# Stage Y of a decoder layer's MLP: Strassen's seven products for the up-projection, in two rounds of 612 tokens

## Chip, core and metric

One NeuronCore of a Trainium2 chip runs the whole program. It has five engines with an instruction stream each: PE (TensorE, matrix products), DVE (VectorE), ACT (ScalarE), POOL (GpSimd) and SP, which here issues nearly all DMAs. The metric is device time in microseconds (us) for one execution; lower is better. All operands and results are fp32.

## What is computed

One decoder layer over 2048 prompt tokens and 8 sample tokens, T = 2056 in all, D = 1024, d_ff = 4096. Attention, pooling and the sample group's caches come first; they are not touched. What matters here is the rest, the same for every token:

```python
hp = hp + _mixer_out(outs, lses, pooled, w_out)        # [A, B] @ w_out
def _mlp(h, g, w_up, w_down):
    a = jax.nn.relu(rmsnorm(h, g) @ w_up)
    return (a * a) @ w_down
hp = hp + _mlp(hp, norm_mlp_g, w_up, w_down)
def _ple(h, p, g, w_gate, w_ple):
    gate = jax.nn.sigmoid(rmsnorm(h, g) @ w_gate)
    return (p @ w_ple) * gate
hp = hp + _ple(hp, p_prompt, ple_norm_g, w_ple_gate, w_ple)
y_prompt = rmsnorm(hp, final_norm_g)
```

## The kernel before

Activations lie transposed, features on the 128 partitions and tokens along the columns. Every fp32 operand is split into a high part (a cast to fp32r, a format that PE reads) and a low part (the value less its high part), and each product is made of three passes, high x high, high x low, low x high (PASSES). `group` runs the passes over the k tiles into one PSUM bank with `mm` (L190).

After the input projection the tokens are worked in two stages. Stage X holds the first 832 tokens (CX, two chunks of 416); stage Y the last 1224 (CY, chunks of 416, 416 and 392). In the order of the program: the output projection of X, mlp of X with part of the attention in the background, the output projection of Y (with the gate's normalised input of X prepared beside it), the gate of X (with the mlp's normalised input of Y, `prep_norm`, beside it, paced in 24 steps), the mlp of Y (with the final norm, transposes and output of X beside it), the gate of Y and its final norm.

`out_proj` takes each tile of xT into one of two buffers (`xr_`), runs a group of 24 matmuls, adds (DVE, L196), stores h1 to DRAM and adds the square to the statistics.

`mlp` runs 8 blocks of 512 hidden features. A block's upward half has 4 feature tiles x 3 chunks, a group of 8 k tiles x 3 passes = 24 matmuls each: 288; ACT empties the bank with a relu (L1344), POOL squares (L196), ACT casts the high part (L1347), DVE subtracts for the low part (L196). Its downward half has 8 output tiles x 3 chunks, groups of 4 x 3 = 12: 288 again; DVE adds each bank to the accumulator `hacc` in SBUF (L196). Weights come through `load_w`: a DMA of 256 KB into the ring `wr` (SP), POOL copies the high part (`pcopy`, L199), DVE subtracts for the low part (L196). w_up and w_down are read once for all of stage Y.

`gate` makes, for each of 8 output tiles and each chunk, a group of 24 matmuls, the sigmoid, the product with `ple`, the sum in `hacc`, its square for the last norm and the scale by final_norm_g. `Final` transposes on PE (L1466), scales on ACT and DVE (L1472, L1474) and stores the output.

What sets the order: instructions are issued in the order of the code, engine by engine; work in the background is a generator, and `Pace` advances it by so many steps for so much matmul work in front. All memory comes from a few arenas of columns (R for fp32r, F for fp32, and "ma", "mb", which change hands).

## Time and profile before

| | us |
|---|---|
| median of 3 runs | 2733.47 (2732.52 to 2735.83) |
| the profiled execution, own time | 2738.41 |
| its span, first to last instruction | 2736.7 |
| mean granted TensorE clock | 0.988 |
| output projection of Y (span time 1545 to 1651) | 106.0 |
| gate of X (1651 to 1740) | 89.0 |
| mlp of Y (1740 to 2603) | 863.0 |
| gate of Y, up to the last matmuls (2603 to 2724) | 121.0 |

The profile is of one execution. Times of an instruction are its recorded duration; on PE such records overlap, since matmuls are pipelined, so how far apart matmuls stand is read from a row that holds many of them without a break. PEld are the loads of weights into PE, one per matmul. In the table of stages each column is an engine's busy time with its count of instructions, then the granted clock as a share of full speed, the DMA engines' mean busy share, and the GB/s moved.

### The profile page before, as it was taken

How to read it: one execution, taken by the hardware profiler on the slowest of the kernel's cores; microseconds unless marked ns; L12 is line 12 of the kernel's file. 1: busy time of each engine (PE TensorE's matmuls, PEld its weight loads, DVE VectorE, ACT ScalarE, POOL GpSimd, SP SyncE). 2: the span in 40 equal slices, each digit the busy share in tenths (PEclk: the TensorE clock that was granted, in tenths of full speed). 3: DMA queues.
4: the chain of work that ended last, by engine and by line, in shares of the span. 5: the costliest groups of instructions: out<-in, count | busy, mean ns of one | idle time of the engine just before them, and what ended most of it. 6: DMA issues, size and time to landing. Idle time of an engine off the chain costs nothing. (4 is left out here: it accounts for less than half of the span.)

```text
span 2736.7 us, 43091 instructions
## 1 busy us (share of the span) xinstructions
PE 2654.8 (97%) x15686; PEld 2533.5 (93%) x15686; DVE 1555.8 (57%) x3373; ACT 847.9 (31%) x1605; POOL 1030.3 (38%) x1354
## 2 busy tenths in 40 slices
PE   8999899998999999999999999999999999999998
PEld 6888899977988999999999898999999999999998
DVE  6747766675587766766775757432332332323675
ACT  6221344453243244242343424301011011011354
POOL 2414645444276443343443725412122122122263
PEclk9999999999999999999999999999999999999999
DMA  7364244477144332332322545431111111111124
GB/s 248 127 181 123 80 131 115 112 214 198 55 132 120 88 88 69 109 104 74 95 73 61 165 147 153 131 104 39 39 39 44 42 39 39 39 39 39 53 84 150
DMA packets 385938, 272.51 MB, mean 100 GB/s; under 512 B 91466, under 2 KB 349205, under 8 KB 385717
## 3 DMA queue, kind: packets, MB, share of 16 engines
q1 hardware_dynamic: 385653, 269.74, 34.1%
q8 instruction: 123, 2.02, 0.3%
q14 instruction: 90, 0.74, 0.1%
q10 hardware_dynamic: 72, 0.02, 0.0%
HBM read 209.47 MB, written 60.30 MB: 99 GB/s over the span
## 5 line engine op out<-in xcount | busy, mean ns | idle before, releaser
L190 PE MATMUL bank<-mem_r 128*128 128x416 f32 (+11 forms) x13608 | 2455.9, 339 | 49.7 <-DVE mem_r L196 11.1
L190 PEld LDWEIGHTS bank<-mem_r 128*128 128x128 f32 (+2 forms) x13608 | 2311.1, 185 | 128.3 <-DVE mem_r L196 18.9
L199 POOL TENSOR_SCALAR mem_r<-mem_f 128x512 fp32r<-128x512 f32 (+1 forms) x444 | 324.9, 736 | 808.3 <-PE bank L190 718.3
L196 DVE TENSOR_TENSOR mem_r<-mem_f,mem_r 128x512 fp32r<-128x512 f32 (+3 forms) x568 | 434.1, 770 | 179.4 <-POOL mem_r L199 139.4
L196 DVE TENSOR_TENSOR mem_f<-bank,mem_f 128x416 f32<-128x416 f32 (+3 forms) x488 | 272.6, 565 | 238.0 <-PE bank L190 228.0
L196 DVE TENSOR_TENSOR mem_r<-mem_mb,mem_r 128x416 fp32r<-128x416 f32 (+6 forms) x236 | 173.6, 743 | 339.6 <-ACT mem_r L1347 312.2
L1344 ACT ACTIVATE mem_mb<-bank 128x392 f32<-128x392 f32 (+1 forms) x160 | 82.3, 515 | 798.5 <-PE bank L190 798.5
L196 POOL TENSOR_TENSOR mem_mb<-mem_mb 128x416 f32<-128x416 f32 (+1 forms) x140 | 143.2, 1023 | 307.1 <-ACT mem_mb L1344 282.6
L776 DVE CUSTOM_DVE_ANT_0 bank<-bank,mask 128x256 f32<-128x256 f32 (+3 forms) x504 | 159.5, 338 | 43.5 <-PE bank L190 39.6
L199 POOL TENSOR_SCALAR mem_r<-mem_r 128x256 fp32r<-128x256 f32 (+1 forms) x117 | 91.5, 795 | 87.8 <-PE bank L190 77.7
L859 POOL TENSOR_SCALAR_AFFINE_SELECT mem_ma<-mem_ma 128x256 f32<-128x256 f32 (+2 forms) x148 | 74.7, 524 | 99.4 <-ACT mem_ma L871 44.6
L196 DVE TENSOR_TENSOR mem_ma<-bank,mem_ma 128x416 f32<-128x416 f32 (+2 forms) x104 | 63.4, 610 | 85.6 <-PE bank L190 70.3
L1347 ACT CAST mem_r<-mem_mb 128x416 fp32r<-128x416 f32 (+1 forms) x128 | 68.5, 535 | 134.2 <-POOL mem_mb L196 134.1
L190 PE MATMUL bank<-mem_mb,mem_r 128*64 128x64 f32 (+4 forms) x494 | 99.9, 321 | 3.1 <-DVE mem_r L196 1.0
L190 PEld LDWEIGHTS bank<-mem_mb,mem_r 128*128 128x128 f32 (+1 forms) x494 | 79.4, 177 | 12.3 <-DVE mem_r L196 1.7
L196 DVE TENSOR_TENSOR mem_r<-mem_ma,mem_r 128x512 fp32r<-128x512 f32 (+4 forms) x88 | 70.8, 809 | 32.4 <-ACT mem_r L880 26.1
L199 POOL TENSOR_SCALAR mem_r<-mem_mb 128x512 fp32r<-128x512 f32 (+3 forms) x61 | 57.2, 946 | 70.6 <-PE bank L190 51.4
L196 POOL TENSOR_TENSOR mem_f<-mem_f 128x416 f32<-128x416 f32 (+2 forms) x52 | 69.2, 1334 | 32.0 <-DMA mem_f<-in_cache_attn_kv_dram 12.5
L776 DVE DVE_READ_ACCUMULATOR2_ANT mem_ma<- 128x1 f32 (+1 forms) x512 | 68.4, 134 | 0.0
L196 POOL TENSOR_TENSOR mem_ma<-mem_ma 128x416 f32<-128x416 f32 (+1 forms) x41 | 52.5, 1289 | 38.3 <-ACT mem_ma L1410 14.4
L196 DVE TENSOR_TENSOR mem_f<-mem_f,mem_ma 128x416 f32<-128x416 f32 (+1 forms) x64 | 47.2, 737 | 26.2 <-ACT mem_ma L1190 11.3
L859 POOL TENSOR_SCALAR_AFFINE_SELECT mem_mb<-mem_mb 128x256 f32<-128x256 f32 (+2 forms) x76 | 33.9, 466 | 56.2 <-ACT mem_mb L868 21.2
(254 smaller groups left out, 1808.9 us busy)
## 6 DMA issues: line engine op xcount, KB each, us to landing
mem_f<-in_w_up_dram SPq DMA_DIRECT2D x128, 256.0 KB
mem_f<-in_w_down_dram SPq DMA_DIRECT2D x128, 256.0 KB
mem_f<-in_w_in_dram SPq DMA_DIRECT2D x64, 256.0 KB
out_dram<-mem_f SPq DMA_DIRECT2D x55, 256.0 KB
mem_f<-in_cache_attn_kv_dram SPq DMA_DIRECT2D x48, 256.0 KB
mem_f<-in_w_ple_gate_dram SPq DMA_DIRECT2D x48, 256.0 KB
mem_f<-in_x_prompt_dram SPq DMA_DIRECT2D x64, 128.0 KB
xT_s<-mem_f SPq DMA_DIRECT2D x32, 256.0 KB
```

What stands on the lines that cost most here:

```text
L190: PE.matmul(out, l, r, start=start, stop=stop)
L196: eng.tensor_tensor(out, a, b, op=op)
L199: G.tensor_scalar(out, src, 1.0, 1.0, op0=ALU.mult, op1=ALU.mult)
L776: V.tensor_tensor_reduce(src, src, mask, 1.0, -3e38, ALU.add, ALU.max, mcol[: src.shape[0], col : col + 1])
L859: G.affine_select(out=p, in_=p, pattern=[[0, nblk], [sign, w]], compare_op=ALU.is_ge, fill=0.0, base=base, channel_multiplier=-sign)
L1344: S.activation(a, ps[:, :ln], AF.Relu)
L1347: S.copy(x[:, 0], sq)
```

## The change

The tokens of stage Y are cut into four chunks of 306 (HY) and worked in two rounds of two chunks, 612 tokens each. In a round, the up-projection treats weights and activations as 2 x 2 halves: the k tiles' upper and lower 512 rows, the hidden features' lower and upper 2048, and the two chunks. Instead of eight products of halves it makes seven of sums and differences (Strassen's scheme in Winograd's form; SEVEN lists operand slots, bank, and product). `upward` does this for 128 hidden features of each half: 7 products x 4 k x 3 passes = 84 matmuls of 306 columns, 16 times per round. Three products open a bank and four add to a bank that holds another; after each, ACT copies the bank (4) or DVE adds it (3) into `z`, four results of 306 columns. Relu, square and cast are three ACT instructions of 1224 columns, the low part one of DVE. `downward` is an ordinary product: 4 output tiles x 2 chunks, 12 matmuls each, 96, 16 times per round. The steps follow one another as `sections` lists them.

`Weights7` loads four blocks of 256 x 128 of w_up (4 DMAs of 128 KB), makes the sums on DVE (`w_sums`, 4 of 256 columns), and the parts: ACT casts and DVE subtracts, 1024 columns at once ("early") and 768 ("late"). `WeightsD` loads w_down, one cast and one subtraction of 1024. Both weights are read once per round, twice in all. `Fill` prepares a step's weights while the step before runs.

Around it: the normalised, summed activations are made by `prep_seven`, four steps of 7 slots x 306, beside the gate of X for round 1 and at the end of round 1 for round 2. The gate of X writes its result to DRAM (hxS) and `final_from` reads it back tile by tile in the first upward steps of round 1. Round 1's result goes to DRAM (h2) and is reloaded. The gate of Y is called for chunks (0, 1), (2) and (3), loading its weights each time. COLS_F gives 832 columns to a new piece "mc", which changes which buffers the first stages draw.

The core of the diff:

```diff
@@ constants
-CY = [(2 * LC, LC), (3 * LC, LC), (4 * LC, T - 4 * LC)]
+HY = NY // 4
+CY = [(NX + i * HY, HY) for i in range(4)]
-COLS_F = 10824
+COLS_F = 9992
+COLS_MC = 832
@@ after mlp
+    SEVEN = ((0, 0, 0, 1), (3, 3, 2, 5), (5, 5, 0, 6), (1, 1, 1, 2), (4, 4, 0, 7), (6, 2, 2, 3), (2, 6, 0, 4))
+    OPENS = (1, 2, 5)
+    def w_sums(raw, s):
+        tt(V, s[:, 0], raw[:, 0], raw[:, 3], ALU.subtract)
+        tt(V, raw[:, 3], raw[:, 3], raw[:, 2], ALU.add)
+        tt(V, s[:, 1], raw[:, 3], raw[:, 0], ALU.subtract)
+        tt(V, s[:, 2], raw[:, 1], s[:, 1], ALU.subtract)
...
+        def early(self):
+            w_sums(self.a, self.b)
+            self.p4 = self.parts(self.a, self.w4, 4)
+        def late(self):
+            self.p3 = self.parts(self.b, self.w3, 3)
+        def parts(self, src, ring, n):
+            w = [x.rearrange("p (s n) -> p s n", s=n) for x in ring()]
+            S.copy(w[0], src)
+            tt(V, w[1], src, f(w[0]), ALU.subtract)
+            return w
...
+        for blk in range(NBLK):
+            for j in range(2):
+                out.append((True, blk, j))
+                if blk:
+                    out.append((False, blk - 1, j))
+        return out + [(False, NBLK - 1, j) for j in range(2)]
...
+        def upward(blk, j):
+            ws = fill.take()
+            z = z_view(zr(4 * ln), 4)
+            for slot_w, slot_z, b, p in SEVEN:
+                n, last = 0, 3 * len(x) - 1
+                for k, xk in enumerate(x):
+                    for i, q in PASSES:
+                        PE.matmul(bu[b][:, :ln], ws[k // 2].at(slot_w, i, k % 2), xk[:, q, slot_z],
+                                  start=n == 0 and p in OPENS, stop=n == last, skip_group_check=p not in OPENS)
+                        n += 1
+                fill.work(12 * ln)
+                ps = bu[b][:, :ln]
+                if p in (1, 5, 6, 4):
+                    S.copy(z[:, {1: 0, 5: 2, 6: 3, 4: 1}[p]], ps)
+                else:
+                    i = {2: 0, 3: 3, 7: 2}[p]
+                    tt(V, z[:, i], ps, z[:, i], ALU.add)
+                if p == 3:
+                    fill.late()
+            S.activation(z, z, AF.Relu)
+            S.activation(z, z, AF.Square)
+            r = rl[blk, j] = z_parts_view(rls(), 4)
+            S.copy(r[:, 0], z)
+            tt(V, r[:, 1], z, f(r[:, 0]), ALU.subtract)
+        def downward(blk, half):
+            ws = fill.take()
+            fill.late()
...
+                                mm(ps[:, :ln], ws[o // 2].at(i, 2 * fh + j, o % 2), rl[blk, j][:, q, AT[fh, ci]], n == 0, n == 11)
+                    hc = hacc[ft].ap[:, ci * ln : ci * ln + ln]
+                    tt(V, hc, ps[:, :ln], hc, ALU.add)
...
@@ stage Y
-    gate(xg, hx, stx.buf.ap, (0, 1), gate_w(wr), Pace(bg, 24, 24 * NX * 7))
+    bg = prep_seven(h1, rst, g_mlp, xs, CY[:2], zr)
+    gate(xg, lambda ft, ci: hx[ft].ap[:, ci * LC : ci * LC + LC], stx.buf.ap, (0, 1), gate_w(wr), Pace(bg, 4, 24 * NX * 7), dump=hxS)
-    mlp(xm, get_acc_y, 512, wr, Pace(bg, 7, 24 * NY * 3.5), before_last_y)
+    bgx = final_from(hxS, finx, tpx)
+    fill = Fill(chain(mlp_steps(), mlp_steps()), rings, None)
+    fill.hook = Pace(bgx, 8, 2 * 7 * 12 * HY * 0.9)
+    hy, st1 = mlp_seven(xs, acc_of(h1, slice(y0, y1)), rls, zring, fill, last_1, keep_1)
+    hy2, st2 = mlp_seven(cur["xs"], acc_of(h1, slice(y1, T)), rls, zring, fill, last_2, lambda *_: None)
-    gate(xg, hy, sums[:, :NX], (0, 1), gate_w(wr), Pace(held["bg"], 9, 24 * NX))
+    gate(xg, where, sums.ap, (0, 1), gate_w(wr), Pace(bg, 16, 24 * 2 * HY * 7))
+    gate(xg, where, sums.ap[:, 2 * HY :], (2,), gate_w(wr, w_more), Pace(bg, 7, 24 * HY * 7))
+    last_gate(xg, hy2, y1, where, sums.ap[:, 3 * HY :], 3, gate_w(wr, w_more), Ring.of(wr.b + yr.b),
+              final(hy2, y1, sums.ap[:, 2 * HY :], y1, y1 + HY, yr), 4)
```

How the engines' rows stand, in three places; a row is a line of the code, an operation, what it writes and reads, and how often in a row.

First, DVE in the middle of stage Y's mlp. Before, bank to `mem_f` is the accumulators' sum, 512 columns a weight's low part, `mem_mb` the squared activations' low part:

```order
L196 TENSOR_TENSOR mem_f<-bank_73,mem_f 128x392
L196 TENSOR_TENSOR mem_r<-mem_f,mem_r 128x512
L196 TENSOR_TENSOR mem_f<-bank_70,mem_f 128x392
L196 TENSOR_TENSOR mem_r<-mem_f,mem_r 128x512
L196 TENSOR_TENSOR mem_r<-mem_mb_15973,mem_r 128x416 x2
L196 TENSOR_TENSOR mem_r<-mem_f,mem_r 128x512 x2
L196 TENSOR_TENSOR mem_r<-mem_mb_15973,mem_r 128x392
```

After, in the middle of a round, 256 columns are a sum of weights, 1024 the low part of four slots or of w_down, bank to `mem_ma` an upward product's sum, bank to `mem_f` an accumulator's:

```order
L199 TENSOR_TENSOR mem_f<-bank_77,mem_f 128x306
L199 TENSOR_TENSOR mem_r<-mem_ma_1834,mem_r 128x1224
L199 TENSOR_TENSOR mem_f<-mem_f 128x256
L199 TENSOR_TENSOR mem_f<-bank_75,mem_f 128x306
L199 TENSOR_TENSOR mem_f<-mem_f 128x256 x2
L199 TENSOR_TENSOR mem_r<-mem_f,mem_r 128x1024
L199 TENSOR_TENSOR mem_f<-mem_f 128x256 x4
L199 TENSOR_TENSOR mem_ma_1834<-bank_72,mem_ma_1834 128x306
L199 TENSOR_TENSOR mem_ma_1834<-bank_74,mem_ma_1834 128x306
```

The preparation of the next weights now stands between the banks' sums, in pieces, where before one subtraction of 512 stood between several sums.

Second, PE where stage Y's mlp begins. Before, groups of 24 follow the gate's without a break, with the ones-products of X's statistics and the transposes of X's result (L1466) between:

```order
L190 MATMUL bank_73<-mem_r 128x416 x12
L190 MATMUL bank_74<-ones_96,mem_f 128x1 x6
L190 MATMUL bank_74<-ones_96,mem_f 64x1
L190 MATMUL bank_73<-mem_r 128x416 x12
L190 MATMUL bank_70<-mem_r 128x416 x24
L1466 MATMUL bank_75<-ident_91,mem_f 128x128 x4
L1466 MATMUL bank_76<-ident_91,mem_f 128x128 x4
```

After, the last two groups of the gate are followed by the first round's products (L1543), whose first matmuls change between three banks:

```order
L193 MATMUL bank_72<-mem_r 128x416 x12
L193 MATMUL bank_74<-mem_r 128x416 x24
L1543 MATMUL bank_71<-mem_r 128x306 x6
L1543 MATMUL bank_72<-mem_r 128x306 x6
L193 MATMUL bank_77<-ones_99,mem_f 128x1 x3
L1543 MATMUL bank_71<-mem_r 128x306 x2
L1543 MATMUL bank_72<-mem_r 128x306 x2
L1543 MATMUL bank_74<-mem_r 128x306 x8
```

The products that come first now need the sums of weights and of activations, where before they needed a weight tile and one normalised tile.

Third, SP's queue there. Before, `h_s` 128x1224 are the accumulators' loads and `out_dram` X's output:

```order
L187 DMA mem_f<-in_w_up_dram 128x4x128 x2
L187 DMA mem_mb_15973<-h_s 128x1224
L187 DMA mem_ma_1831<-ple_s 128x416
L187 DMA mem_f<-in_w_up_dram 128x4x128 x2
L187 DMA mem_ma_1831<-h_s 128x1224 x2
L187 DMA out_dram<-mem_f 128x512 x4
L187 DMA mem_f<-in_w_down_dram 128x2x256 x3
L187 DMA out_dram<-mem_f 128x512 x2
```

After, `hx_s` is X's result, written and read back:

```order
L190 DMA mem_f<-in_w_up_dram 128x2x128 x3
L190 DMA mem_f<-hx_s 128x8x128 x2
L190 DMA mem_f<-in_w_up_dram 128x2x128
L190 DMA hx_s<-mem_f 128x416
L190 DMA mem_f<-in_w_up_dram 128x2x128 x3
L190 DMA mem_f<-in_w_down_dram 128x2x256 x2
L190 DMA mem_f<-h_s 128x612 x2
L190 DMA mem_f<-hx_s 128x8x128
L190 DMA out_dram<-mem_f 128x512 x2
```

Reads of X's result, loads of accumulators, weights and stores of the output now take turns in one queue, where before X's result stayed in SBUF.

## Rows read from the trace of the kernel before

**Rows 1.** The page: span, engines' busy time, granted clock, GB/s.
```profile
span 2736.7 us, 43091 instructions
...
PE 2654.8 (97%) x15686; PEld 2533.5 (93%) x15686; DVE 1555.8 (57%) x3373; ACT 847.9 (31%) x1605; POOL 1030.3 (38%) x1354
...
PEclk9999999999999999999999999999999999999999
...
GB/s 248 127 181 123 80 131 115 112 214 198 55 132 120 88 88 69 109 104 74 95 73 61 165 147 153 131 104 39 39 39 44 42 39 39 39 39 39 53 84 150
```

**Rows 2.** Busy time by stage: stretch, us, engines, clock, DMA share, GB/s.
```profile
1545.00:1651.00 106.00, 102.76 (x572) 99.97 (x571) 60.60 (x105) 28.27 (x53) 35.02 (x34) 1.00 0.45 138
1651.00:1740.00 89.00, 81.96 (x425) 78.44 (x425) 63.98 (x81) 41.96 (x76) 55.51 (x50) 0.98 0.50 150
1740.00:1856.20 116.20, 115.29 (x651) 114.10 (x650) 42.04 (x71) 20.80 (x38) 23.73 (x30) 1.00 0.33 108
1856.20:2496.50 640.30, 640.30 (x3458) 635.74 (x3457) 195.76 (x312) 75.27 (x145) 135.76 (x168) 1.00 0.13 40
2496.50:2603.00 106.50, 106.46 (x586) 105.02 (x585) 55.10 (x94) 31.66 (x60) 32.67 (x36) 1.00 0.15 44
2603.00:2680.00 77.00, 74.96 (x401) 72.99 (x400) 58.30 (x74) 38.06 (x68) 48.19 (x45) 1.00 0.33 94
2680.00:2724.00 44.00, 42.78 (x275) 41.66 (x274) 24.05 (x39) 19.76 (x34) 16.80 (x18) 1.00 0.52 162
```

**Rows 3.** Timeline of PE: start, us, unbroken rows of matmuls.
```profile
403.57 2.49 PE L190 MATMUL bank<-mem_r 128*128 128x264 f32 x19
...
67.73 7.85 PE L190 MATMUL bank<-mem_r 128*128 128x512 f32 x33
```

**Rows 4.** PE by line and form, whole run: busy us, mean ns.
```profile
L190 PE MATMUL bank<-mem_r 128*128 128x512 f32 x672 | 176.2, 404 | 3.8 <-POOL mem_r L199 1.7 <-DVE mem_r L196 1.0 <-ACT mem_r L1164 0.6
...
L190 PE MATMUL bank<-mem_r 128*128 128x264 f32 x432 | 65.2, 289 | 2.7 <-DVE mem_f L1170 2.4 <-DVE mem_r L196 0.3
...
L190 PE MATMUL bank<-mem_r 128*128 128x64 f32 x256 | 32.6, 276 | 0.0
```

**Rows 5.** By line and form, 1856.2 to 2496.5 us.
```profile
L190 PEld LDWEIGHTS bank<-mem_r 128*128 128x128 f32 x3457 | 636.0, 188 | 4.6
...
L196 DVE TENSOR_TENSOR mem_r<-mem_f,mem_r 128x512 fp32r<-128x512 f32 x96 | 66.1, 689 | 52.7 <-POOL mem_r L199 51.8
...
L196 DVE TENSOR_TENSOR mem_f<-bank,mem_f 128x416 f32<-128x416 f32 x60 | 35.5, 592 | 91.3 <-PE bank L190 91.3
...
L1347 ACT CAST mem_r<-mem_mb 128x416 fp32r<-128x416 f32 x48 | 25.9, 540 | 47.6 <-POOL mem_mb L196 47.6
```

**Rows 6.** DVE by line and form, whole run.
```profile
L196 DVE TENSOR_TENSOR mem_r<-mem_f,mem_r 128x512 fp32r<-128x512 f32 x468 | 377.2, 810 | 151.4 <-POOL mem_r L199 138.5 <-PE bank L190 3.6 <-ACT mem_r L1107 3.0
...
L196 DVE TENSOR_TENSOR mem_f<-bank,mem_f 128x256 f32<-128x256 f32 x32 | 13.1, 410 | 0.4 <-PE bank L190 0.2
```

**Rows 7.** ACT by line and form, whole run.
```profile
L880 ACT CAST mem_r<-mem_ma 128x512 fp32r<-128x512 f32 x44 | 27.4, 623 | 17.6 <-POOL mem_ma L859 17.5
```

**Rows 8.** Timeline of the output projection of Y: one buffer's turn.
```profile
1603.69 0.32 SPq L187 DMA_DIRECT2D mem_ma<-xT_s  x1
...
1606.98 0.59 DVE L196 TENSOR_TENSOR mem_ma<-bank,mem_ma 128x416 f32<-128x416 f32 x1 [2.67 <-DMA mem_ma<-xT_s]
...
1614.88 0.52 SPq L187 DMA_DIRECT2D h_s<-mem_ma  x1
...
1617.68 0.32 SPq L187 DMA_DIRECT2D mem_ma<-xT_s  x1
```

**Rows 9.** Waits, 1500 to 1760 us: us in total, times, longest us.
```profile
DVE mem_ma L196 <- DMA mem_ma<-xT_s: 15.3, 7, 3.6
```

More of the change, by code (lines that the diff above doesn't have):

```diff
@@ L1184, in __init__ @@
             self.acc = [self.buf.ap[:, c0 - chunks[0][0] : c0 - chunks[0][0] + ln] for c0, ln in chunks]
-            self.sq = Ring(F, 2, LC)
+            self.sq = Ring(F, nsq, max(ln for _, ln in chunks))
         def add(self, ft, ci, src):
@@ L1218, in prep_norm @@
     def prep_norm(src, rs, gc, xa, cis):
-        tr = Ring(F, 3, LC)
+        tr = Ring(F, 3, max(ln for _, ln in xa.chunks))
         for ci in cis:
@@ new lines, in decoder_step, with __init__, early, late @@
+    class Fill:
+        def __init__(self, steps, rings, hook):
+            self.steps, self.rings, self.hook, self.ready, self.open = iter(steps), rings, hook, [], None
+            self.early()
+            self.late()
+        def early(self):
+            step = next(self.steps, None)
+            if step is None:
+                return
+            ws = [kind(self.rings) for kind, _ in step]
+            for w, (_, at) in zip(ws, step):
+                w.load(*at)
+                w.early()
+            self.open = ws
+        def late(self):
+            if self.open is None:
+                return
+            for w in self.open:
+                w.late()
+            self.ready.append(self.open)
+            self.open = None
+        def take(self):
+            ws = self.ready.pop(0)
+            self.early()
+            return ws
+        def work(self, n):
+            if self.hook:
+                self.hook(n)
@@ L1395, in load_acc, with gate @@
         return acc
-    def gate(xa, hacc, sums, cis, getw, hook, step=None):
-        base, s0 = xa.chunks[0][0], xa.chunks[cis[0]][0]
-        sr, pr = Ring(F, 2, LC), Ring(F, 2, LC)
+    def gate(xa, where, sums, cis, getw, hook, step=None, dump=None):
+        s0 = xa.chunks[cis[0]][0]
+        width = max(xa.chunks[ci][1] for ci in cis)
+        sr, pr = Ring(F, 2, width), Ring(F, 2, width)
         for ft in range(KD):
@@ L1444, in add_up @@
         def add_up(self, ps, src, start, stop):
-            order = range(len(self.tiles))
-            for i in order if start(0) else reversed(order):
+            order = sorted(range(len(self.tiles)), key=lambda i: -self.tiles[i][1])
+            self.widest = order[0]
+            for i in order if start(order[0]) else reversed(order):
                 p, rw = self.tiles[i]
@@ L1492, in final, with final_from, last_gate @@
             yield
-    def last_gate(xa, hacc, base, sums, ci, getw, yr, bg, nbg):
+    def final_from(src, fin, tp):
+        hr, yr = Ring(F, 2, KD * P), Ring(F, 2, 512)
+        for i, (p0, rw) in enumerate(fin.tiles):
+            fin.hacc = hr().rearrange("p (k c) -> p k c", k=KD)
+            dma(fin.hacc[:, :, :rw], src[:, p0 - fin.p0 : p0 - fin.p0 + rw].rearrange("(k p) c -> p k c", p=P))
+            psa = [tp(), tp()]
+            for ft in range(KD):
+                fin.turn(i, ft, psa[ft // 4])
+            for dh in range(2):
+                fin.give(i, dh, psa[dh], yr())
+            yield
+        for x in (hr, yr):
+            x.free()
+    def last_gate(xa, hacc, base, where, sums, ci, getw, yr, bg, nbg):
         c0, ln = xa.chunks[ci]
-        fin = Final(hacc, base, sums, c0, c0 + ln)
+        fin = Final(hacc, base, c0, c0 + ln)
         full = len(fin.tiles) - 1
@@ L1520, in step @@
                     fin.give(full, dh, b[1 - dh], yr())
-        gate(xa, hacc, sums, (ci,), getw, Pace(bg, nbg, 24 * ln * (KD - 3)), step)
+        gate(xa, where, sums, (ci,), getw, Pace(bg, nbg, 24 * ln * (KD - 3)), step)
     xa = [Acts(IN_PART[0], keys=("ma", "mb", "r"), high=True), Acts(IN_PART[1])]
@@ L1586, in decoder_step @@
     mp, tp = Turns([bank[0], bank[1], bank[3]]), Turns([bank[2]])
-    hx = [F.alloc(NX, ("f",)) for _ in range(KD)]
+    hx += [F.alloc(NX, ("f",)) for _ in range(KD - 1)]
     st = Stat(CX, tp)
@@ new lines, in decoder_step, with __init__, __call__ @@
+    wf = Ring.of([F.alloc(1024, ("f",)) for _ in range(3)]), Ring.of([F.alloc(768, ("f",)) for _ in range(2)])
+    rings = (*wf, w4, w3)
+    tpx = Turns([bank[2], bank[7]])
+    tp = tpx
+    bgx = final_from(hxS, finx, tpx)
+    fill = Fill(chain(mlp_steps(), mlp_steps()), rings, None)
+    cur = {}
+    class Cols:
+        def __init__(self, ring):
+            self.ring = ring
+        def __call__(self, cols):
+            return self.ring()[:, :cols]
+    zring = Cols(Turns([b.ap for b in zr.b]))
@@ L1673, in decoder_step, with where @@
+    for ft in range(KD):
+        dma(hy[ft].ap, h2[ft * P : ft * P + P])
+    wr = Ring(F, 4, 512)
+    sums = F.alloc(NY)
     more = Region(R, (4 * 2048, "r", False))
     w_more = Ring.of(w_ring.b + Ring(more, 4, 2048).b)
-    sums = held["st"].buf.ap
-    gate(xg, hy, sums[:, :NX], (0, 1), gate_w(wr), Pace(held["bg"], 9, 24 * NX))
-    drain(held["bg"])
+    def where(ft, ci):
+        return (hy, hy2)[ci // 2][ft].ap[:, ci % 2 * HY : ci % 2 * HY + HY]
+    mp, tp = Turns([bank[0], bank[1], bank[3]]), Turns([bank[2], bank[4], bank[5], bank[6], bank[7]])
```

261 lines of the change are left out of this document (208 added, 53 removed).

## The prediction

> **What bounds the kernel now.** I read the page's head first: TensorE is busy for 97% of the span and its granted clock is at the upper of its two levels (2.4 GHz) in all forty slices, so the clock is no term here [rows 1]. Next comes busy time by stage. In the 640.3 us that hold six blocks of stage Y's mlp, PE is busy for all 640.3, DVE for 196, ACT for 75, POOL for 136, and the DMA share is 0.13 [rows 2]. Nothing but the number and the length of the matmuls sets that stage. Around it, the output projection and the two gates have PE at 92 to 97%, with DVE at 55 to 76% and DMA at 0.33 to 0.52 [rows 2]: there other work is close behind.
>
> A matmul's price is its distance from the next one, not its recorded duration, because records overlap. Six blocks hold 6 x 576 = 3456 matmuls, so 640.3 / 3456 = 185.3 ns each, at 408 columns in the mean (two chunks of 416, one of 392) [rows 2]. From unbroken rows of the timeline, a row's length less one matmul's own time, over the count less one: 264 columns (2.49 - 0.289) / 18 = 122.3 ns, 512 columns (7.85 - 0.404) / 32 = 232.7 [rows 3, 4].
>
> **The change, part by part.** *Matmuls of the mlp.* Before: 8 blocks x 106.7 us = 853.7 us for 4608 matmuls. After: each of two rounds has 16 upward steps of 7 x 4 x 3 = 84 and 16 downward ones of 96, so 2 x 16 x 180 = 5760 matmuls of 306 columns. In columns that is 1.76 M against 1.88 M, 6.3% less. No row has 306. Between 264 (122.3) and 408 (185.3) a straight line gives 140.7; the line through 408 and 512, carried down, gives 138.8; a bare share of the 408 price gives 139.0 and a bare share of the 264 price 141.8. I take 140, between the two lines: 806.4 us, **-47.3 us**. Ends: 138.8 gives -54.2, 141.8 gives -36.9.
>
> *Output projection and gate of Y.* 1152 matmuls at 185.3 = 213.5 us become 1536 at 140 = 215.0: **+1.6** (ends -0.3 and +4.3).
>
> *Vector work in the rounds.* Two DVE rows, 256 columns at 410 ns and 512 at 689 [rows 6 and 5], give 131 + 1.09 per column (416: 584 worked out, 592 measured [rows 5]). An upward step then has 8 sums of 256 (3.3 us), two subtractions of 1024 (2.5) and two of 768 (1.9), 3 adds of 306 (1.4) and one subtraction of 1224 (1.5): 10.6 us. A downward step has two subtractions of 1024 and 8 adds: 6.2 us. A pair asks 16.8 us of DVE. ACT by two cast rows (416: 540 ns [rows 5], 512: 623 [rows 7]) is 180 + 0.865 per column: 9.3 + 2.1 = 11.4 us. PE needs 180 x 140 = 25.2 us a pair. So the cover holds: DVE would have to run 1.5 times slower, and the most that this trace shows is 810 against 689, 1.18 times (POOL and ACT at work beside it), which makes 19.7 us [rows 5, 6]. POOL gives up its copies and squares: nothing on the path. The weights are read twice now; a pair moves 2 MB in 25 us, 83 GB/s, against 40 now, while gate X alone moved 150 GB/s at half the DMA engines' time [rows 2]. I cost all this at **0**; what a failure costs stands under the third rival.
>
> *Start of round 1.* Here three things meet that were apart. (a) DVE: the first step's weights need 2 x (1.6 + 1.2 + 1.0) = 7.7 us, the second's early parts 5.8 more, 13.5 together, while PE's cover is the last two groups of gate X, 48 x 190 = 9.1 us: **+4**. (b) DMA: X's result goes to DRAM and comes back (3.4 MB read, 3.4 MB of output written), the accumulators are loaded (2.5 MB) and three steps' weights (3.1 MB), 12.4 MB in all; half the share at 150 GB/s [rows 2] means some 300 GB/s full, so 41 us, while the three upward steps ahead of the first downward one last 3 x 84 x 140 = 35.3: **+6**. Those transfers stand in SP's one queue ahead of later weights, so a late one holds the products, not only X's output. Ends for both: 0, and +20 if (b) also holds up the next weights.
>
> *Ring of the output projection.* Two buffers take xT in, the sum, and h1 out. The trace shows 3.3 us from a load's issue to the add, 0.6 for the add, and 2.8 from the store's issue to the next load's [rows 8]: 6.7 us per buffer, so one group per 3.35 us. A group of Y lasts 24 x 185.3 = 4.45 us now and DVE already waits 15.3 us for these loads in all [rows 9]. With 306 columns a group lasts 3.36 us: level with the ring. 32 groups: 0 to 12 us, I take **+3**, near the low end, since the sum leaves no deficit and only jitter is left.
>
> *Ends of the rounds and gate Y.* Statistics of 4 chunks instead of 3, gate weights loaded three times instead of two, reloads of h2: **+4** (0 to 8; the rows nearest are the gate stages, where PE lost 7.0, 2.0 and 1.2 us [rows 2]). The part ahead of stage Y is not meant to change, but the smaller buffer for eight load tiles shifts its order a little: 0, +-4.
>
> *Sum.* -47.3 + 1.6 + 4 + 6 + 3 + 4 = **-28.7 us**. Against the profiled run's own 2738.4 us that is 2709.7; that run stood 4.9 above the median of 2733.5, so the median of after should be **2705**.
>
> **Rivals.** *First, all is covered.* If the starts and the ring cost nothing: -47.3 + 1.6 + 4 = -41.7, 2692. For it: gate X and mlp X hid as much movement elsewhere. Against: three demands in the same 35 us.
>
> *Second, congestion at the seams is larger.* The ring at +12 and the start at +20 instead of +10: -28.7 + 19 = -9.7, 2724. For it: these are the only stages where PE now waits [rows 2].
>
> *Third, slower: DVE takes PE's place in the rounds.* The upward products use three banks in turn; each waits for DVE or ACT to empty its bank, and on DVE the emptying stands behind the preparation of coming weights. A product lasts 12 x 140 = 1.7 us, so a bank has 3.4 us of cover where products follow each other; two weights' sums and 1024-wide subtraction in a row take 2 x 2.9 = 5.8 us, which would hold PE 2.4 us in every pair: 32 x 2.4 = 77 us, 2782. It decides against the change from 0.9 us a pair (28.7 / 32). Against it: the order on DVE puts emptyings between the pieces; the longest stretch without one is six sums and one 1024-wide subtraction, 6 x 0.41 + 1.25 = 3.7 us, and there upward products alternate with downward groups, which have three banks of their own, so that a bank's cover is over 3.4. For it: late weights on SP's queue would shift just this.
>
> *Fourth, loads of weights become the bound.* Weight loads are busy for 635.7 of the 640.3 us, 184 ns each [rows 2, 5]. If each load kept that time, 5760 would take 1060 us instead of 854 (+206), and the 1536 of the projection and the gate 283 instead of 213.5 (+69); with the seams' 17 that is 3025. But a row of 264-column matmuls goes at 122.3 ns each with a load for each [rows 3], and 256 matmuls of 64 columns took 32.6 us, 127 ns each [rows 4]: the load record stretches to fill the matmul's time. The Trainium skill (Perfetto Trace Analysis, section Identifying the Most-Contended Engine) says to judge TensorE's headroom by how busy its weight loads are and not by how busy its matmuls are; by that, 99% here would leave nothing to win from shorter matmuls, only from fewer. The trace disagrees at 264 columns, so it gets a small chance.
>
> *That the change does not do what it says* has next to none: the order has 2 x 16 x 84 product rows and 2 x 16 x 96 downward ones.
>
> **How the numbers follow.** Better than the first rival 0.04; first rival (2687 to 2697) 0.20; my forecast (2697 to 2715) 0.52; second rival (2715 to 2732) 0.14; third 0.08; fourth 0.02. The range, 2687 to 2728, runs from the low side of the first rival to most of the second, leaving out about 2 in 10. About 0.2%, 5.5 us, is what a measurement of this kernel tells from no change: faster (below 2728) 0.86, same 0.05, slower 0.09.
>
> **What would show it.** 7296 matmuls of 306 columns at 139 to 142 ns apart; PE above 99% inside the rounds with DVE near 67%, ACT near 45%, POOL near nothing, 83 GB/s; a round of some 403 us; PE's waits gathered in the first 40 us of round 1 and, in the output projection, behind DVE waiting for xT. I am wrong if a pair takes over 26 us, if the matmuls stand over 143 ns apart, or if the seams cost over 30 us.

## The result: slower by 1.3%, and where the time went

The changed kernel took 2768.68 us (median of 4 runs, 2765.55 to 2776.12), the kernel before 2734.65 (4 runs); the ratio is 1.013, with a 95% interval of 1.0114 to 1.0147. The forecast of 2705 was wrong, and its sign too.

The head of the page of the changed kernel, to be read against [rows 1]: PE's busy time fell by 17 us, as the shorter product promised, while the span grew by 30, and the clock is no longer at its upper level in every slice (the two slices with an 8, against none before).

```profile
span 2766.9 us, 47611 instructions
...
PE 2638.0 (95%) x17242; PEld 2515.2 (91%) x17242; DVE 1821.9 (66%) x3902; ACT 1118.2 (40%) x1910; POOL 859.5 (31%) x1163
...
PEclk9999999999999999999999899999999899999999
...
GB/s 240 140 167 126 88 123 132 110 211 197 39 167 115 62 91 106 66 113 88 70 82 95 130 115 171 198 123 72 92 85 87 161 84 75 86 92 89 129 121 164
```

By stage, the table of busy time of the changed kernel (columns as in [rows 2]: stretch, us, PE, PEld, DVE, ACT, POOL, clock, DMA share, GB/s). The rows are: output projection of Y, gate of X, start of round 1, round 1, its end, the change of rounds, round 2.

```profile
1535.00:1665.00 130.00, 113.26 (x745) 110.68 (x746) 66.13 (x134) 30.38 (x65) 34.41 (x35) 0.92 0.44 122
1665.00:1745.00 80.00, 75.55 (x388) 72.14 (x387) 54.44 (x75) 39.63 (x66) 37.17 (x33) 0.98 0.54 163
1745.00:1790.00 45.00, 37.25 (x245) 35.92 (x246) 31.78 (x56) 25.37 (x38) 7.05 (x4) 0.89 0.73 227
1790.00:2130.00 340.00, 338.38 (x2395) 337.36 (x2395) 204.10 (x343) 148.80 (x180) 0.00 (x0) 1.00 0.32 96
2130.00:2165.00 35.00, 33.54 (x234) 32.86 (x234) 24.95 (x44) 16.82 (x22) 3.18 (x2) 1.00 0.39 114
2165.00:2210.00 45.00, 27.92 (x152) 24.42 (x151) 32.12 (x61) 19.20 (x34) 8.82 (x6) 0.73 0.55 167
2210.00:2550.00 340.00, 339.11 (x2396) 338.10 (x2396) 206.24 (x351) 149.78 (x183) 0.00 (x0) 1.00 0.27 83
```

Inside the rounds nearly all is as forecast: PE busy over 99%, DVE 60% (67 was forecast), ACT 44%, POOL at nothing, 83 to 96 GB/s, the clock at its upper level. The loss is at the seams: in the output projection PE is idle for 17 of 130 us (before, 3 of 106 [rows 2]), and at the change of rounds for 17 of 45 us, with the clock at 0.73.

Stage lengths, each from the first matmul of a stage to the first of the next in the profiled execution, for both kernels and all experiments (us; the ratio is to the kernel before, with its interval). The two rounds, whose matmuls are interleaved where they meet, are parted in the middle, at the 2880th of their 5760 matmuls:

| kernel | output proj. Y | gate X | mlp of Y | gate Y to the end | ratio |
|---|---|---|---|---|---|
| before | 115.6 | 84.6 | 865.4 | 135.5 | |
| changed | 141.4 | 81.8 | 432.3 + 436.8 | 152.8 | 1.0130 (1.0114 to 1.0147) |
| e1_op416 | 113.2 | 85.8 | 430.7 + 438.9 | 152.6 | 1.0070 (1.0054 to 1.0085) |
| e2_ring4 | 131.0 | 90.1 | 431.5 + 438.7 | 153.4 | 1.0144 (1.0127 to 1.0161) |
| e3_norm_ahead | 142.7 | 82.0 | 439.1 + 416.5 | 154.0 | 1.0098 (1.0083 to 1.0113) |
| e4_keep_gate_w | 137.9 | 82.2 | 434.3 + 438.2 | 151.5 | 1.0136 (1.0121 to 1.0151) |
| e5_before_mc | 115.6 | 85.9 | 866.9 | 135.0 | 0.9991 (0.9978 to 1.0004) |
| e6_op416_ahead | 114.3 | 86.6 | 438.0 + 418.1 | 153.1 | 1.0025 (1.0016 to 1.0035) |
| e7_late_stat | 115.0 | 84.7 | 439.7 + 418.2 | 153.5 | 1.0031 (1.0017 to 1.0045) |
| e8_no_norm_in_gate | 142.4 | 81.5 | 432.6 + 436.9 | 142.3 | one execution, no ratio |
| e9_by_chunk | 116.0 | 85.8 | 438.7 + 425.5 | 146.4 | 1.0010 (0.9999 to 1.0022) |
| e10_dump_on_act | 137.3 | 82.4 | 431.4 + 439.1 | 153.5 | 1.0131 (1.0111 to 1.0151) |
| e11_all_repairs | 115.9 | 87.6 | 435.3 + 425.8 | 147.1 | 1.0020 (1.0009 to 1.0031) |

From before to changed that is +25.8, -2.8, +3.7 and +17.3: 44.0 us. The mlp, where 47 us were to be won, won nothing, since what its matmuls saved was lost at its start and between the rounds; the stages on both sides lost 40. The two spans differ by only 30.2, because the profiled execution of the changed kernel came to stage Y 13.7 us sooner. Of that, 4.8 us lie in X's projection and mlp, and 8.9 us in the stretch before them. e5 tells what the 8.9 are worth.

The theory tested here: the seven products do in the rounds what was forecast, and the loss is four separate seams (output projection, start of round 1, change of rounds, gate of Y), each a chain of dependent steps that got less PE work to hide under. The rival: DVE has more to do now and is what limits the seams as a whole, so that a repair of one only moves the wait to the next.

### The profile page after: what moved, and what is told of

Its sections match the earlier page's. It is cut to its first block, busy times and chain, and to the rows that moved or that the text cites. A ratio compares the mean times of both kernels' runs of the same rounds, so it can differ in the third digit from the quotient of the medians.

```text
span 2766.9 us, 47611 instructions
## 1 busy us (share of the span) xinstructions
PE 2638.0 (95%) x17242; PEld 2515.2 (91%) x17242; DVE 1821.9 (66%) x3902; ACT 1118.2 (40%) x1910; POOL 859.5 (31%) x1163
## 4 chain that ended last, share of the span: by engine, by line
PE 33%; DVE 6%; DMA 4%; issue 3%; ACT 2%; POOL 2%; SPq 0%; DVEq 0%; POOLq 0%; ACTq 0%
PE bank L193 19%; PE bank L1543 13%; DVE mem_r L199 2%; DVE mem_f L199 1%; DVE mem_ma L199 1%; POOL mem_ma L199 1%; DMA mem_ma<-in_w_ple_gate_dram 1%; DVE mem_r L1236 1%; DMA mem_ma<-h_s 1%; POOL mem_r L202 1%; DMA mem_f<-in_w_up_dram 1%; DMA h_s<-mem_ma 0%; PE bank L1711 0%; POOL mem_f L199 0%; DVE mem_mb L199 0%
## 5 line engine op out<-in xcount | busy, mean ns | idle before, releaser
L193 PE MATMUL bank<-mem_r 128*128 128x306 f32 (+10 forms) x11496 | 1984.0, 323 | 54.0 <-DVE mem_r L199 17.7
L193 PEld LDWEIGHTS bank<-mem_r 128*128 128x128 f32 (+2 forms) x11496 | 1793.4, 184 | 127.5 <-DVE mem_r L199 27.9
L199 DVE TENSOR_TENSOR mem_r<-mem_f,mem_r 128x512 fp32r<-128x512 f32 (+6 forms) x538 | 456.7, 859 | 163.6 <-POOL mem_r L202 74.2
L199 DVE TENSOR_TENSOR mem_f<-bank,mem_f 128x306 f32<-128x306 f32 (+4 forms) x590 | 304.2, 521 | 140.8 <-PE bank L193 132.4
L202 POOL TENSOR_SCALAR mem_r<-mem_f 128x512 fp32r<-128x512 f32 x284 | 209.9, 744 | 444.6 <-PE bank L193 337.3
L1543 PE MATMUL bank<-mem_r 128*128 128x306 f32 x1504 | 238.0, 308 | 17.9 <-ACT mem_r L1420 13.1
L1543 PEld LDWEIGHTS bank<-mem_r 128*128 128x128 f32 x1504 | 221.4, 191 | 21.3 <-ACT mem_r L1420 14.0
L193 PE MATMUL bank<-mem_r,mem_mb 128*128 128x306 f32 (+1 forms) x992 | 216.1, 303 | 5.3 <-DVE mem_mc L782 3.1
L1543 PE MATMUL bank<-mem_r,mem_mb 128*128 128x306 f32 x992 | 172.9, 305 | 0.9 <-ACT mem_ma L1549 0.7
L193 PEld LDWEIGHTS bank<-mem_r,mem_mb 128*128 128x128 f32 x992 | 164.8, 189 | 6.5 <-DVE mem_mc L782 3.5
L199 DVE TENSOR_TENSOR mem_ma<-bank,mem_ma 128x306 f32<-128x306 f32 (+1 forms) x160 | 82.2, 514 | 132.6 <-PE bank L1543 79.8
L1543 PEld LDWEIGHTS bank<-mem_r,mem_mb 128*128 128x128 f32 x992 | 150.3, 190 | 2.5 <-ACT mem_ma L1549 2.5
L202 POOL TENSOR_SCALAR mem_r<-mem_r 128x256 fp32r<-128x256 f32 (+1 forms) x117 | 90.2, 783 | 81.8 <-PE bank L193 73.7
```

The lines of the kernel that those rows point to most:

```text
L193: PE.matmul(out, l, r, start=start, stop=stop)
L199: eng.tensor_tensor(out, a, b, op=op)
L202: G.tensor_scalar(out, src, 1.0, 1.0, op0=ALU.mult, op1=ALU.mult)
L1543: PE.matmul(bu[b][:, :ln], ws[k // 2].at(slot_w, i, k % 2), xk[:, q, slot_z], start=n == 0 and p in OPENS, stop=n == last, skip_group_chec ...
```

## Experiments: the output projection of Y

In the changed kernel two things stand out there. In the list of waits (engine, line, what it waited for: us in total, times, longest), from 1522 to 1664 us, DVE waits for xT two and a half times as long as before [rows 9], and PE once waits 6.3 us for the small operations of a statistic (that of one of stage X's chunks: 4 x 104 = 416 columns):

```profile
DVE mem_ma L199 <- DMA mem_ma<-xT_s: 37.9, 19, 4.2
...
PE bank L1211 <- DVE tiny L199: 6.3, 1, 6.3
```

The timeline shows the second one: PE's sums over partitions (products with ones), then nothing until the transposes of the result (L1211); between them lie a reciprocal root on ACT and DVE and the subtractions queued on DVE. That wait is a third of what PE waits for in the stage, 18.4 us in all.

```profile
1533.87 0.81 PE L193 MATMUL bank<-ones,mem_f 128*104 128x1 f32 x8
...
1540.98 0.96 PE L1211 MATMUL bank<-ident,tiny 104*128 104x104 f32 x4 [6.30 <-DVE tiny L199]
```

**e1_op416** takes back the short chunks in the projection alone:

```diff
+CO = [(2 * LC, LC), (3 * LC, LC), (4 * LC, T - 4 * LC)]
-    cat = Acts(CY)
+    cat = Acts(CO)
-    st = Stat(CY, tp)
+    st = Stat(CO, tp)
```

> The changed kernel, with the output projection of Y and its statistics in the old chunks of 416, 416 and 392 again; the mlp's two rounds and the gate keep chunks of 306. If the shorter groups are what makes the output projection of Y 141 us long instead of 116, it falls back to 115 to 120 us and the whole run to about 2745. If the loss there only comes from another order of the instructions around it (the statistics of stage X, the gate's preparation), it stays above 130 us and the run above 2758.

The stage took 113.2 us, 28 less, and the ratio fell from 1.013 to 1.007: the run gained 16 us, and 2753 is not the 2745 expected. In the two traces the gate of X is 4.0 us longer and Y's projection begins 9.3 us later. Busy time in the whole stage, in the changed kernel and in e1, and the timeline at the same statistic:

```profile
1521.85:1663.28 141.43, 122.80 (x818) 119.92 (x817) 77.69 (x145) 36.56 (x79) 46.64 (x46) 0.93 0.45 123
```

```profile
1531.10:1644.30 113.20, 111.69 (x622) 109.66 (x622) 70.42 (x116) 32.06 (x61) 44.03 (x41) 1.00 0.47 138
```

```profile
1544.74 0.81 PE L194 MATMUL bank<-ones,mem_f 128*104 128x1 f32 x8
1545.41 6.34 PE L194 MATMUL bank<-mem_r 128*128 128x392 f32 x33
1551.60 0.52 PE L1212 MATMUL bank<-ident,tiny 104*128 104x104 f32 x4
```

Now 33 matmuls, 6.3 us, stand between the sums and the transposes, and PE is idle for 1.5 us of the stage instead of 18.6. PE's busy time fell too, by 11 us, of which the matmuls' number and length explain 1.6; most of the rest is matmuls at the lower clock (0.93 in the stage before this edit, 1.00 after). DVE is busy for a larger share of the shorter stage (70.4 of 113.2 us, against 77.7 of 141.4), so a full DVE is not what PE waited for. The order of PE's instructions, which was known before the run, has this difference. First the changed kernel, then e1:

```
L193 MATMUL bank_73<-ones_99,mem_f 104x1 x4
L1211 MATMUL bank_73<-ident_94,tiny_7143 128x104 x4
L193 MATMUL bank_73<-ones_99,mem_f 104x1 x4

L194 MATMUL bank_73<-ones_99,mem_f 104x1 x4
L194 MATMUL bank_72<-mem_r 128x392 x14
L194 MATMUL bank_71<-mem_r 128x416 x19
L1212 MATMUL bank_73<-ident_94,tiny_7143 128x104 x4
```

The other traces agree: in the six kernels with short chunks in the projection PE waits 5.5 to 6.9 us at this statistic, in the five with the old chunks 0.6 at the most. But e1 gives the ring more time as well (DVE's waits for xT fall to 9.5 us), so it does not part the two by itself.

**e2_ring4** leaves the chunks and widens the ring, the term that the prediction had named:

```diff
-        xr_ = None if acc else Ring(F, 2, LC)
+        xr_ = None if acc else Ring(F, 4, HY)
```

> The changed kernel, with four buffers of 306 columns instead of two of 416 for xT and h1 in the output projection of Y. If the two-buffer ring is the cause (a group every 3.36 us against 3.35 us per buffer pair, DVE waiting 37.9 us for xT), DVE's wait for xT falls under 10 us and the run gets 15 to 25 us shorter. If DVE's own queue or the statistics are, the wait goes but the run gets under 8 us shorter.

DVE's wait for xT fell from 37.9 to 13.8 us, not to under 10 as expected, and the stage by 10.4 us; but the gate of X grew by 8.3, and the run did not get faster (ratio 1.0144). The two waits that remain, from 1522 to 1653 us for DVE and to 1745 us for PE:

```profile
DVE mem_ma L199 <- DMA mem_ma<-xT_s: 13.8, 7, 3.3
```

```profile
PE bank L1211 <- DVE tiny L199: 14.5, 2, 8.7
```

The wait of 5.8 us at the first statistic is still there, and the stage, at 131.0 us, is still 18 us longer than in e1: the ring was a cost, but not the larger part. The second wait, of 8.7 us, is new and stands near the start of the gate of X. The statistic there has 31 matmuls between its two parts, as in the changed kernel, where PE waits 0.7 us at it; but its root on ACT (at 1671.88) stands behind an activation of round 1's preparation, and that waits for POOL and a load of h1:

```profile
1668.61 1.37 POOL L199 TENSOR_TENSOR mem_ma<-mem_ma 128x612 f32<-128x612 f32 x1 [14.99 <-DMA mem_ma<-h_s]
...
1670.02 0.55 ACT L1497 ACTIVATE mem_ma<-mem_ma,gcols 128x306 f32<-128x306 f32 x1 [10.56 <-POOL mem_ma L199]
```

Here the rival is half right: what one edit saves can be lost in the next stage, though by the order in a queue and not by DVE's load (56.6 us of work in this gate, 56.1 in the changed kernel's).

## Experiments: the change of rounds

The rows of the timeline of the changed kernel for one of the four steps that make round 2's activations (loads from h1, the factor per token on POOL, the factor per feature on ACT, sums on DVE, casts L1420):

```profile
2157.49 0.96 ACT L1420 CAST mem_r<-mem_ma 128x918 fp32r<-128x918 f32 x1
...
2160.59 0.79 SPq L190 DMA_DIRECT2D mem_ma<-h_s  x2
...
2167.57 1.92 POOL L199 TENSOR_TENSOR mem_ma<-mem_ma 128x612 f32<-128x612 f32 x1 [12.34 <-DMA mem_f<-in_w_up_dram]
...
2169.52 0.55 ACT L1497 ACTIVATE mem_ma<-mem_ma,gcols 128x306 f32<-128x306 f32 x1 [4.38 <-POOL mem_ma L199]
...
2172.29 1.25 ACT L1497 ACTIVATE mem_ma<-mem_ma,gcols 128x612 f32<-128x612 f32 x2 [1.87 <-POOL mem_ma L199]
...
2173.80 0.94 ACT L1420 CAST mem_r<-mem_ma 128x918 fp32r<-128x918 f32 x1
```

All four steps share one buffer; their first casts stand at 2157.49, 2173.80, 2191.06 and 2202.83, and the last cast of all ends at 2207.5. The last upward products of round 1 end at 2138.6, and the downward work behind them lasts 3 x 96 x 141 ns = 41 us, to about 2180. So PE runs out of work. The chain also begins late. The first step's features were loaded before the last upward products, but its factors per token (`rst_s`) only right after DVE's subtraction for the last upward step's result; the code puts them where that result's buffer was:

```profile
2122.57 2.62 SPq L190 DMA_DIRECT2D mem_ma<-h_s  x4
...
2148.88 0.81 SPq L190 DMA_DIRECT2D mem_ma<-rst_s  x2
```

```profile
2147.43 1.43 DVE L199 TENSOR_TENSOR mem_r<-mem_ma,mem_r 128x1224 fp32r<-128x1224 f32 x1
...
2152.04 1.65 POOL L199 TENSOR_TENSOR mem_ma<-mem_ma 128x612 f32<-128x612 f32 x1 [383.33 <-DMA mem_ma<-rst_s]
```

PE's own rows:

```profile
2182.85 0.56 PE L1543 MATMUL bank<-mem_r 128*128 128x306 f32 x2 [1.06 <-DVE mem_r L199]
2192.06 0.88 PE L1543 MATMUL bank<-mem_r 128*128 128x306 f32 x2 [8.65 <-ACT mem_r L1420]
...
2205.08 1.39 PE L1543 MATMUL bank<-mem_r 128*128 128x306 f32 x4 [0.38 <-DVE mem_r L199]
2206.46 2.23 PE L1543 MATMUL bank<-mem_r,mem_mb 128*128 128x306 f32 x8
...
2209.38 1.30 PE L1543 MATMUL bank<-mem_r 128*128 128x306 f32 x8
```

**e3_norm_ahead** takes both factors out of the chain: POOL and ACT apply them during round 1, in columns that are spare then, and store the result to DRAM (`zn`).

```diff
+                tt(G, x, x, rb, ALU.mult)
+                S.activation(x, x, AF.Copy, scale=g_mlp[:, k : k + 1])
+                dma(zn[k * P : k * P + P, t * HY : t * HY + HY], x)
-        cur["bg"] = prep_seven(h1, rst, g_mlp, cur["xs"], CY[2:], ...)
+        cur["bg"] = prep_seven(zn, None, None, cur["xs"], CY[2:], ..., True)
```

> The changed kernel, with round 2's activations normalised during round 1 into DRAM (in spare columns, 16 pieces, POOL and ACT), so that the steps between the rounds have only load, sums and parts left: a chain of about 10 us instead of 15, four times, against 40 us of matmuls. If the serial chain in one buffer is what PE waits for at the start of round 2 (23 us), that wait falls to 0 to 8 us and the run to about 2750. If DVE's total work at this place is (it is busy for 71% there), the wait falls by less than 6 us.

Round 2 took 416.5 us instead of 436.8. The change of rounds and what follows, by busy time:

```profile
2155.00:2190.00 35.00, 35.00 (x250) 35.00 (x249) 33.69 (x62) 18.92 (x25) 0.00 (x0) 1.00 0.74 212
2190.00:2235.00 45.00, 41.13 (x288) 39.64 (x288) 33.63 (x70) 26.67 (x41) 0.00 (x0) 1.00 0.42 127
```

PE is busy for all of the first 35 us while DVE is busy for 96% of them, and for 41 of the next 45: DVE's total work was not the cause, the chain was. The trace shows in which way, and it is not the way expected. The first loads of e3's four steps, from SP's queue (the other two at 2162.55 and 2178.51):

```profile
2136.51 1.76 SPq L190 DMA_DIRECT2D mem_ma<-zn_s  x4
...
2146.71 9.20 SPq L190 DMA_DIRECT2D mem_ma<-zn_s  x4
```

From step to step these are 10.2, 15.8 and 16.0 us; in the changed kernel (2122.57, 2160.59, 2176.70, 2193.24) 38.0, 16.1 and 16.5. So the later steps did not get shorter without their factors. What went is the wait for the factors at the head: e3's first cast comes 9.5 us before round 1's last upward products end, the changed kernel's 18.9 us after. Round 1 pays 6.8 us, more than was expected, so the run gained 8 us and not some 19 (ratio 1.0098). It pays at its start: in its first 100 us, where the work moved into it begins, PE is idle for 17.2 us instead of 9.3.

## Experiments: the gate of Y

**e4_keep_gate_w** loads the gate's weights twice instead of three times:

```diff
+    def kept_w(ft):
+        if ft not in kept:
+            kept[ft] = gate_w(wr, w_more)(ft)
+        return kept[ft]
```

> The changed kernel, with the gate's weights of the third call kept in eight buffers for the fourth, so that they are loaded and split twice instead of three times. If weights per group (2 loads of 256 KB, two copies on POOL, two subtractions on DVE for every 3.4 us of matmuls) are what makes the gate of Y 153 us instead of 136, it falls by 6 to 12 us. If the statistics and the last norm are, by under 3 us.

The second and third call together, in the changed kernel and then in e4:

```profile
2682.20:2754.10 71.90, 68.19 (x480) 67.27 (x481) 49.64 (x85) 33.18 (x65) 35.33 (x44) 0.95 0.60 179
```

```profile
2684.90:2755.60 70.70, 67.14 (x480) 65.90 (x481) 34.28 (x69) 34.52 (x65) 21.54 (x28) 0.98 0.42 123
```

DVE and POOL lost 15 and 14 us of work, the DMA share a third, and the stretch 1.2 us. The third loading of the weights costs nothing that can be measured.

**e8_no_norm_in_gate** looks at the first call, beside which round 2's 612 tokens are normalised. It leaves that normalisation out; the gate of those tokens reads round 1's activations instead:

```diff
-    bg = prep_norm(lambda k, ci, t: where(k, ci), lambda ci: st2.acc[ci - 2], g_ple, xg, (2, 3))
+    for k in range(KD):
+        xg.b[k, 2], xg.b[k, 3] = xg.b[k, 0], xg.b[k, 1]
+    bg = iter(())
```

> The changed kernel, leaving out the normalisation of round 2's tokens for the gate (their gate reads round 1's activations instead), which stands beside the gate's first call (54 us of matmuls, DVE busy for 78%). If that crowding is what makes the first call take 68 us, it falls to 56 to 60 us and its waits to under 3 us; if the weights or the two PSUM banks of the later calls are, it stays above 64 us.

The first call, in the changed kernel and in e8:

```profile
2614.10:2682.20 68.10, 60.19 (x416) 58.72 (x415) 51.25 (x80) 32.26 (x68) 40.15 (x44) 0.97 0.32 91
```

```profile
2616.30:2674.70 58.40, 57.45 (x416) 57.19 (x414) 32.16 (x61) 25.72 (x53) 25.79 (x33) 1.00 0.38 106
```

It fell by 9.7 of the 14 us that it had over its matmuls (384 x 141 ns = 54 us). The kernel before ran its last block of the mlp chunk by chunk, so that much of this normalisation stood beside the mlp; the changed kernel's downward steps alternate the two chunks, so both statistics are ready only when the mlp has ended.

**e9_by_chunk** puts that back, on top of the repairs of e1 and e3 (which are e6, below): round 2's last block does its first chunk for all output tiles, then the second, with the first chunk's normalisation beside it.

```diff
+            for ci in range(2):
+                for ft in range(KD):
...
+                    if ci and ft == 0:
+                        st.finish(0)
+                        between(hacc)
```

> The kernel with the two repairs (old chunks in the output projection, round 2's activations normalised ahead), and round 2's last downward block worked chunk by chunk, as the kernel before works its last block, so that half of the normalisation for the gate stands beside the last 96 matmuls instead of beside the gate's first call. If that normalisation is what makes the gate's first call 68 us instead of 54, the call falls to 60 to 64 us and the run from 2740 to 2732 to 2736, level with the kernel before. If the work only moves the waits into the end of round 2, the run stays at 2738 to 2743.

The gate's first call took 61.9 us, against 68.3 in e6, and the gate 6.7 us less in all; but round 2 grew by 7.4 in the trace, so what the gate won there came back ahead of it: in the last 100 us of round 2 PE is idle for 7.4 us, in e6 for 2.0. Over all runs the ratio fell from 1.0025 to 1.0010, with an interval that holds 1: level with the kernel before.

## Experiments: the sum, the start of round 1, and the lead

**e6_op416_ahead** is e1 and e3 together.

> The changed kernel with two repairs together: the output projection of Y in chunks of 416, 416 and 392, and round 2's activations normalised ahead in round 1. If the two losses are independent seams, their gains add: 16 us and 8 us off 2769, so 2742 to 2748, and the two rounds together take some 855 us. If what is saved at one seam is lost at the next, 2750 to 2758.

2740.0 us, ratio 1.0025: the gains added (29 us together, 16 and 8 apart, which is the same within the intervals). The two rounds took 856.1 us, 9.3 less than the mlp before, so the seven products do win once the seam between the rounds is covered. In the middle of round 1 PE has no idle time:

```profile
1800.00:2130.00 330.00, 330.00 (x2336) 329.87 (x2336) 199.63 (x337) 145.69 (x179) 7.54 (x8) 1.00 0.32 99
```

**e7_late_stat** goes from e6 and moves the sums for X's last norm, which stand among round 1's first products, to the first tile that is read back:

```diff
-    finx.add_up(ps, stx.buf.ap, lambda i: True, lambda i: True)
-    finx.rstd(ps)
+    S.copy(sumx.ap, stx.buf.ap)
```

> As the kernel with the two repairs, and the sums for X's last norm (products with ones, which stand in PE's queue among round 1's first products and wait for the gate's tail) are issued with the first tile that is read back. If that wait (4.7 us in the changed kernel, and the lower clock behind it) is PE's queue order, the start of round 1 gets 5 to 8 us shorter. If DVE's preparation of the first weights is what is late, the wait moves to the products and nothing is gained (under 2 us).

Round 1 took 439.7 us against 438.0: nothing won. The wait moved to the products, which now wait for a cast of the weights (timeline of PE):

```profile
1734.48 2.92 PE L1545 MATMUL bank<-mem_r 128*128 128x306 f32 x10 [5.30 <-ACT mem_r L1452]
```

**e10_dump_on_act** tests, on the changed kernel, whether that cast is late because the weights' loads stand on SP's queue behind the stores of X's result:

```diff
-                    dma(dump[ft * P : ft * P + P, c0 - s0 : c0 - s0 + ln], hc)
+                    S.dma_start(dump[ft * P : ft * P + P, c0 - s0 : c0 - s0 + ln], hc)
```

> The changed kernel, with the sixteen stores of X's result issued from ACT's queue instead of SP's, so that the first weights of round 1 no longer stand behind stores that wait for the gate's last results. If SP's queue order is what makes the first products wait (8.6 us of waits and 4.0 us at the lower clock between 1745 and 1790 us), the first 45 us of round 1 get 4 to 10 us shorter. If DVE and ACT are busy with the gate's tail and the preparation, they get under 2 us shorter or longer, since ACT issues the stores.

Round 1 took 431.4 us against 432.3, and the ratio is 1.0131 against 1.0130. The place of those stores in the queue is not the cause.

**e11_all_repairs** has e9's edits, e10's, and the normalisation ahead starting later in round 1.

> All repairs together: old chunks in the output projection, round 2's activations normalised ahead (starting some eight steps later in round 1), the last downward block of round 2 chunk by chunk, and X's result stored from ACT's queue. The kernel with the first three stands at 2737, level with the kernel before. If the start of round 1 (round 1 takes 438 us with the normalisation ahead, 431 without) can be had back, round 1 takes 424 to 432 us and the run 2722 to 2731, the first version faster than the kernel before (2733 to 2735). If not, 2734 to 2740.

Round 1 took 435.3 us, 3.4 less than in e9 but not the 424 to 432 hoped for, and the run 2739.4 (ratio 1.0020): no better than e9. No version here beats the kernel before.

**e5_before_mc** is the kernel before with only the memory split of the change:

```diff
-COLS_F = 10824
+COLS_F = 9992
+COLS_MC = 832
```

> The kernel before, with nothing of the change but the split of memory: COLS_F 9992 and a piece of 832 columns from which the first stages draw two of eight load tiles, one constant buffer and the first accumulator. The changed kernel reached stage Y's output projection 13.7 us earlier than the kernel before. If the split of memory is why, this kernel gets there 8 to 14 us earlier too and ends at 2720 to 2726; if that lead is the run's own scatter, it ends at 2730 to 2737.

2731.25 us, ratio 0.9991 with an interval that holds 1: the split is worth nothing that can be measured. Its profiled execution reached X's projection at 655.1 us, the kernel before at 665.7; but e6 and e7, whose programs are alike up to there, reached it at 665.2 and 656.8. So the early lead of 8.9 us in the changed kernel's trace is scatter between single executions, and the stage lengths are what can be compared. X's projection and mlp together take 864 to 870 us in the thirteen traces, so the other 4.8 us are no more than that.

## Why the prediction was wrong, step by step

- *Matmuls of the mlp, -47.3.* Right in kind, a little short in size. From the timeline of the changed kernel, in a round and in the projection:

```profile
2140.11 7.62 PE L193 MATMUL bank<-mem_r 128*128 128x306 f32 x53
```

```profile
1551.04 13.70 PE L193 MATMUL bank<-mem_r 128*128 128x306 f32 x95
```

  With a matmul's 0.308 us taken off, 7.31 / 52 = 140.6 and 13.39 / 94 = 142.5 ns; over the middle of round 1 in e6, 330 us / 2336 = 141.3. The straight line between 264 and 408 columns (140.7) was the right one; 140 was taken, and the 1.3 ns cost 5760 x 1.3 = 7.5 us.
- *Vector work in the rounds, 0.* Right in the middle of the rounds: DVE 60%, PE busy over 99%. The third rival, DVE taking PE's place there, is refuted.
- *Fourth rival, loads of weights.* Refuted: 337.36 us for 2395 loads is 141 ns each, against 184 before; the record stretches and shrinks with the matmul. The Trainium skill (Perfetto Trace Analysis, section Identifying the Most-Contended Engine) judges TensorE's headroom by MFU, the share of the peak arithmetic, and by how busy the weight loads are. By the second, 99% would have said that there was none; the trace of the rounds disagrees.
- *Start of round 1, +10.* Right in size: 45 us for 245 matmuls and transposes that ask some 35. That is luck, since the two terms of the sum, DVE's weights (+4) and the DMAs (+6), are not what PE waits for there, from 1740 to 1800 us:

```profile
PE bank L193 <- DVE mem_f L199: 4.5, 1, 4.5
PE bank L1543 <- ACT mem_ma L1650: 2.5, 2, 2.3
...
PE bank L1711 <- DMA mem_f<-hx_s: 0.7, 1, 0.7
PE bank L1543 <- DVE mem_r L199: 0.3, 1, 0.3
```

  The first is the sums for X's last norm, the second the gate's sigmoid, which empties the banks that the products need; the clock is 0.89. What sets the start stays open. Neither the sums (e7) nor the stores on SP's queue (e10) do it alone; with the sums moved, the products wait for the gate's tail and for the preparation of the first weights on ACT and DVE, and these were not taken apart further.
- *Ring of the output projection, +3.* The step that failed first. The stage lost 25.8 us. The ring did bind (37.9 us of DVE's waits), and somewhat more than was worked out: the loads at 1603.69 and 1617.68 [rows 8] are two turns of one buffer apart, so a turn is 7.0 us and not 6.7, and a group 3.5 us against 3.36 of matmuls. Widening it won 10.4 us in the stage and nothing in the run. The larger part came with the chunks of 306 in another way: in the order of that version a statistic of 6 us has no matmuls between its two PE parts, PE waits elsewhere in the stage too, and behind the waits the clock falls. The prediction counted matmuls and loads of this stage and none of its statistics. How the 28 us divide among these was not measured.
- *Ends of the rounds and gate Y, +4.* The step that failed most: the change of rounds cost some 20 us (e3) and the gate's first call 10 (e8). The account ahead of the prediction lists `prep_seven` as four steps, but no term of the sum holds when they can begin (with their factors, 10 us after the last upward products) and how long they take (59 us from there to the end of the last cast), against the 41 us of work that cover them. Nor did it notice that the chunk-by-chunk last block was gone. Of what it did price there, the weights loaded three times cost nothing that can be measured (e4).
- *The part ahead, 0.* Right: its lead in the trace is scatter (e5, e6 and e7).
- *Second rival, congestion at the seams.* The right kind. Its price stopped at 2724 because it only stretched the ring and the start; the waits that no term held made the difference.

## What to carry over

When a change leaves the steady state bound by the same engine and only makes its work less, price the seams first: for every chain that must end before the new stage can start, when its first step can begin (which buffer and which factors it waits for) and its latency per step times the steps that share a buffer, against the matmul time that covers it. Then read, in the order of the instructions, what stands between the two parts of every fixed chain: here a statistic of some 6 us had 33 matmuls to hide under with the old chunks and none with the short ones. A repair at one seam is only worth what the next seam lets through: two repairs brought 29 us of 34, and three made the change level with what was there, not faster.
